# One streaming encoder step on one core: later streams in the stick-breaking attention, zero rows by VectorE, own buffers for the merge's first loads, and a re-cut final norm

## The chip, the cores and the metric

One core of a Trainium2 chip runs the whole program. Times are device microseconds (us) of that core. TensorE (PE) does the matmuls and the transposes, VectorE (DVE), ScalarE (ACT) and GpSimd (POOL) do the element work, SyncE (SP) and also ACT and POOL issue DMAs. "Fill" below is matmul work that is ready at any time and is dealt out between dependent steps so that TensorE has something to do.

## What is computed

The reference is one layer of an encoder on 1024 prompt frames and on 8 running streams of 16 new frames each (1152 rows of width 1024 in all):

```python
h = rmsnorm(x); u, va, q, k, vb = split(h @ w_in)      # 512 columns each
a = gelu(u) * (tril(w_s) @ rmsnorm(gelu(va)) + b_s)    # spatial gating, chunks of 128
z = q @ k.T / 8                                        # 8 heads of 64; streams also see 256 cached frames
log_keep = where(mask, log_sigmoid(-z), 0)             # strictly causal
between = reverse_cumsum(log_keep) - log_keep
o = where(mask, exp(log_sigmoid(z) + between), 0) @ v  # stick-breaking, no softmax
x += concat(rmsnorm(a), rmsnorm(o)) @ w_out            # the merge
x += mem_attention(rmsnorm(x))                         # 4 heads of 256, 256 memory rows
x += (silu(h2 @ w_gate) * (h2 @ w_up)) @ w_down        # hidden 2816
y = rmsnorm(x)
```

The projected k and v, the memory keys and values and the streams' normed va rows are outputs too.

## The kernel before

Every float32 matrix is split into a high and a low part (`split`, L121: an ACT cast and a DVE subtraction), and each product is three matmuls (`mm3`, L129). The rows stand in nine tiles of 128 (`NT`); tile 8 holds the streams' 128 rows. The program is written in stages, and the framework orders each engine's instructions by its own plan, near to the order in which they are written; each engine then runs its own list strictly in that order.

**Start and projections** (L208 to L380). Weights and x are loaded, x is normed and turned, and k, v, q and the two gating parts are projected. `head_in(h)` (L190) loads the operands of one attention head from scratch DRAM; for the first two heads it also writes zeros into the half of `qz` that the head does not use (L194).

**Attention** (L385 to L736). Three sources of work are interleaved:

- *Prompt chunks* (`pair`, `chunk`, `sticks`): 8 heads of 12 chunks, 96 in all. A chunk is a chain: two matmuls into `z` on PE, two sigmoids on ACT, a scan on DVE (L417), a product on POOL (L419), transposes on PE (L403), a split on ACT and DVE, and for each pair of chunks the matmuls into `av` (L472). The sum of `av`'s two halves goes to DRAM from the single-buffered tile `oe` (L476 to L479) through SP.
- *Streams* (`stream`, L509): one for each of the 8 running streams, with the same chain in plain float32, and then `stream_tails` (L554), which adds the part of the new frames: four DVE products (L560), eight float32 matmuls, eight DVE sums (L571), and a store (L573). While a stream is in its last matmuls it stands in the list `held`.
- *Fill*: `memory()` (L598), which projects the memory rows, and then `merge_a()` (L634), which computes the first half of the merge, rows of `a_d` times `w_out`. `merge_a` loads a tile's rows of `a_d` into `ar` (L640), transposes them (`prep`), and runs 24 matmuls for each row tile (accumulators `acc`, whose sums are L684). It may not start a `prep` while `held` is not empty, and then hands the turn back (`yield 1`).

`tasks()` (L700) brings the chunks and the streams in order: stream b enters when `S0 + 10 b` chunks have entered, the tails at `S0 + 80`, and the loads of stream b at `S0 + 10 (b - 1) + 8`. The loop that deals the turns counts PE cost by its own rule (`mm`: columns, at least 256, for float32r, and twice the doubled columns for float32; 261 for a transpose) and adds fill until a pass has cost `SLOT` = 4700 counts:

```python
for task in tasks():
    spent[0] = 0
    active.insert(0, task)
    active = [g for g in active if next(g, g) is not g]
    while spent[0] < SLOT:
        if next(fill, 1):
            break
```

A second loop of the same form (L729) drains what is left after the last task. Each pass lets every active chunk and stream take one step.

The outputs of `memory()` go through the tile `mo` (tag "mo", two buffers, L629), which `ar` shares in this kernel.

**Merge, memory attention, feed-forward** (L740 to L1295). The second merge half (`merge_in`, `merge`) starts with loads of `gmem` (L136) and `xt` (L753).

**End** (L1297 to L1351). The down projection runs in six rounds over the nine row tiles, two column halves of 512 each (accumulator `pd`, tag "tr", all eight PSUM banks), summed into `xr` (L1335). In the last round each half is also squared and summed by ACT into `ss` (L1340, its elementwise output is thrown away), POOL turns the two sums into the factor r (L1347, L1348), DVE multiplies the second half by the gain `gfin` (L1349), and `final` (L1312) scales and stores the tile: the first half by DVE (L1316), the second by ACT (L1319).

Of the kernel before, what the change touches and what calls it, by code (L numbers as in the profile page):

```python
# [9 lines left out]
F32 = mybir.dt.float32  # L10
F32R = mybir.dt.float32r
AF = mybir.ActivationFunctionType
ALU = mybir.AluOpType
# [3 lines left out]
P = 128  # L17
# [20 lines left out]
def stream_step(ctx: ExitStack, tc: tile.TileContext, I, O, cst):  # L38
# [14 lines left out]
    def nm(s):  # L53
        uid[0] += 1
        return f"{s}_{uid[0]}"
# [134 lines left out]
    def head_in(h):  # L190
        e, c2 = h % 2, h // 2
        es = slice(e * 64, e * 64 + 64)
        if h < 2:
            nc.gpsimd.memset(qzs[e][64 - e * 64:128 - e * 64].bitcast(F32), 0.0)  # L194
        nc.sync.dma_start(qzs[e][es].bitcast(F32), q_d[c2, 1, es, 0:NP])
        qhh = bhp.tile([P, NP], F32R, tag="qhh", name=nm("qhh"))
        khl = bhp.tile([P, NP], F32R, tag="khl", name=nm("khl"))
        for n in range(2):
            half = slice(n * 64, n * 64 + 64)
            nc.sync.dma_start(khl[half].bitcast(F32), k_d[c2, n ^ e, es, 0:NP])  # L200
            nc.sync.dma_start(qhh[half].bitcast(F32), q_d[c2, 0, es, 0:NP])
        if e == 0:
            vhl = bhp.tile([P, 8, 2, P], F32R, tag="vhl", name=nm("vhl"))
            nc.sync.dma_start(vhl.bitcast(F32), v_d[:, h:h + 2, :].rearrange("(n p) e d -> p n e d", p=P))
            vhls.append(vhl)
        got[h] = qhh, qzs[e], khl, vhls[-1]
# [178 lines left out]
    with ExitStack() as st:  # L385
# [248 lines left out]
        def merge_a():  # L634

            xs = tmp_.tile([P, 2, D], F32, tag="mt", name="xs2")
            aT = tmp_.tile([P, 2, 2, 4, P], F32R, tag="mt", name="aT2")

            def load(i):
                ar = mp.tile([P, 512], F32, tag="mo", name=nm("ar"))  # L640
                nc.sync.dma_start(ar, a_d[i * P:(i + 1) * P, :])
                xt = xs[:, i % 2]
                nc.sync.dma_start(xt, rows(x_p, x_s, i))
                return i, ar, xt

            def prep(i, ar, xt):
                tr = ps("tr", [P, 4, P])
                for c in range(4):
                    tp_(tr[:, c, :], ar[:, c * P:(c + 1) * P], ident)
                ah, al = aT[:, i % 2, 0], aT[:, i % 2, 1]  # L650
                split(ah, al, tr)
                return xt, ah, al

            ins = [load(0), load(1)]
            ws[19] = mem_split(19, raws.pop(19), pend)
            yield 1
            split(*pend.pop())
            yield 1
            while held:
                yield 1  # L660
            cur = prep(*ins.pop(0))
            yield 1
            for i in range(NT):
                xt, ah, al = cur
                if i in (1, 3, 5, 7):
                    raws[20 + i // 2] = mem_load(20 + i // 2)
                elif i in (2, 4, 6, 8):
                    ws[19 + i // 2] = mem_split(19 + i // 2, raws.pop(19 + i // 2), pend)
                for half in range(2):
                    pa = ps("acc", [P, 512])  # L670
                    cnt = 0
                    for c in range(4):
                        wh, wl = ws[16 + c]
                        for lh, rh in ((ah, wh), (ah, wl), (al, wh)):
                            mm(pa, lhsT=lh[:, c, :], rhs=rh[:, half, :], start=cnt == 0, stop=cnt == 11)
                            cnt += 1
                            if cnt % 2 == 0:
                                yield
                            if cnt >= 6 and cnt % 2 == 0 and half == 1 and ins and ins[0][0] == i + 1 and not held:
                                cur = prep(*ins.pop(0))  # L680
                            if cnt == 6 and half == 0 and pend:
                                split(*pend.pop())
                    hs = slice(half * 512, (half + 1) * 512)
                    nc.vector.tensor_tensor(out=xt[:, hs], in0=pa, in1=xt[:, hs], op=ALU.add)  # L684
                yield
                if ins and ins[0][0] == i + 1:
                    while held:
                        yield 1
                    cur = prep(*ins.pop(0))
                nc.scalar.dma_start(xa_d[i * P:(i + 1) * P, :], xt)  # L690
                if i + 2 < NT:
                    ins.append(load(i + 2))

        S0 = 4
        SLOT = 4700
        ZC = 1
        LAG = 2
# [303 lines left out]
    with ExitStack() as stE:  # L1001
# [310 lines left out]
        def final(i, r, xg):  # L1312
            for half in range(2):
                hs = slice(half * 512, (half + 1) * 512)
                if half == 0:
                    nc.vector.scalar_tensor_tensor(out=xr[i][:, hs], in0=xr[i][:, hs], scalar=r, in1=gfin[:, hs], op0=ALU.mult, op1=ALU.mult)  # L1316
                    nc.sync.dma_start(rows(y_p, y_s, i)[:, hs], xr[i][:, hs])
                else:
                    nc.scalar.activation(xr[i][:, hs], xg[:, hs], AF.Copy, scale=r)  # L1319
                    nc.scalar.dma_start(rows(y_p, y_s, i)[:, hs], xr[i][:, hs])  # L1320

        for c, fs in enumerate(chunks):
# [3 lines left out]
            for i in range(NT):  # L1326
# [3 lines left out]
                for half in range(2):  # L1330
                    hs = slice(half * 512, (half + 1) * 512)
                    pd = ps("tr", [P, 512])
                    for n, (hid, wd) in enumerate(now):
                        mm3(pd, hid[:, 0, tsl], hid[:, 1, tsl], wd[:, 0, hs], wd[:, 1, hs], n == 0, n == len(now) - 1)
                    nc.vector.tensor_tensor(out=xr[i][:, hs], in0=pd, in1=xr[i][:, hs], op=ALU.add)  # L1335
                    if last:
                        if half == 0:
                            junk = jp.tile([P, D], F32, tag="w", name=nm("junk"))
                            ss = sm(2)
                        nc.scalar.activation(junk[:, hs], xr[i][:, hs], AF.Square, scale=1.0 / 32, accum_out=ss[:, half:half + 1])  # L1340
                if loads and i % 2 == 1:
                    have.append(prep(*loads.pop(0)))
                if last:
                    if sums:
                        final(i - 1, *sums.pop())
                    tot, r = sm(), sm()
                    nc.gpsimd.tensor_scalar(out=tot, in0=ss[:, 0:1], scalar1=ss[:, 1:2], scalar2=EPS, op0=ALU.add, op1=ALU.add)  # L1347
                    nc.gpsimd.tensor_tensor(out=r, in0=tot, in1=mhalf[:, 0:1], op=ALU.pow)  # L1348
                    nc.vector.tensor_tensor(out=junk[:, hs], in0=xr[i][:, hs], in1=gfin[:, hs], op=ALU.mult)  # L1349
                    sums.append((r, junk))  # L1350
        final(NT - 1, *sums.pop())  # L1351

# [41 lines left out]
```

## Time and profile before

| | us |
| --- | --- |
| runs of the kernel before | 1740.65, 1745.07, 1749.17 (median 1745.07) |
| the profiled execution, its own time | 1748.1 |
| the profiled execution, its span | 1746.2 |

The span runs from the first to the last instruction in the trace; what lies around it in that execution is 1.9 us. Mean granted TensorE clock over the span: 0.989 of 2.4 GHz. By the windows of the trace the projections end near 288 us, the attention near 570, the second merge half near 635, the feed-forward's first products near 1463, and the rest is the down projection and the final norm. The runs shown differ by up to 0.5% of the time.

### The profile page before, as it was taken

The numbers are of one execution on the slowest core, as the hardware profiler recorded it, in microseconds if no ns is written. First come the engines' busy times: TensorE is split into PE (matmuls) and PEld (weight loads), VectorE is DVE, ScalarE is ACT, GpSimd is POOL, SyncE is SP. The second block draws the span as 40 slices with busy tenths as digits, with TensorE's granted clock in tenths as the row PEclk, the third lists the DMA queues.
The fourth block names the chain that finished last, engine by engine and source line by source line (L and its number), as shares of the span: only waits on it lengthen the run. The fifth ranks groups of instructions, "written<-read, shape, count | busy, mean of one in ns | idle before, by whom it ended". The sixth has DMA issues, their size and how long they took to land. (4 is left out here: it accounts for less than half of the span.)

```text
span 1746.2 us, 26290 instructions
## 1 busy us (share of the span) xinstructions
PE 1689.4 (97%) x10039; PEld 1499.7 (86%) x10039; DVE 982.0 (56%) x1479; ACT 676.7 (39%) x1328; POOL 431.8 (25%) x574
## 2 busy tenths in 40 slices
PE   8999999998999999999899899999999999999997
PEld 5889887777777799998788899999999999788886
DVE  5312354888778746545635865555554556444444
ACT  5322234776556436545522523323322233011123
POOL 2101223544333220000001254444444432000002
PEclk9999999999998999999899999999999999999999
DMA  8548145567744534443833232222222237222202
GB/s 272 160 163 278 61 157 170 178 201 210 210 133 159 158 110 125 126 126 113 283 109 108 68 100 70 75 70 72 76 76 77 76 102 264 103 103 103 102 13 97
DMA packets 178253, 229.51 MB, mean 131 GB/s; under 512 B 12176, under 2 KB 125456, under 8 KB 178128
## 3 DMA queue, kind: packets, MB, share of 16 engines
q1 hardware_dynamic: 146432, 163.46, 31.0%
q10 hardware_dynamic: 23504, 35.79, 5.6%
q0 software_dynamic: 8192, 28.58, 4.3%
q8 instruction: 80, 1.31, 0.3%
q14 instruction: 45, 0.37, 0.1%
HBM read 163.43 MB, written 64.36 MB: 130 GB/s over the span
## 5 line engine op out<-in xcount | busy, mean ns | idle before, releaser
L1199 PE MATMUL pp<-b,wg 128*128 128x288 f32 x1584 | 221.4, 296 | 3.4 <-ACT wg L126 2.3
L1199 PEld LDWEIGHTS pp<-b,wg 128*128 128x128 f32 x1584 | 213.5, 188 | 4.3 <-ACT wg L126 2.5
L131 PE MATMUL tr<-wd,hid 128*128 128x512 f32 x396 | 154.7, 391 | 1.2 <-DVE wd L127 1.2
L132 PE MATMUL tr<-wd,hid 128*128 128x512 f32 x396 | 154.1, 389 | 0.0
L130 PE MATMUL tr<-wd,hid 128*128 128x512 f32 x396 | 151.4, 389 | 0.0
L127 DVE TENSOR_TENSOR wg<-s,wg 128x512 fp32r<-128x512 f32 x88 | 87.8, 1000 | 99.5 <-ACT wg L126 86.4
L1335 DVE TENSOR_TENSOR xr<-tr,xr 128x512 f32<-128x512 f32 x108 | 73.2, 689 | 122.2 <-PE tr L132 116.5
L419 POOL TENSOR_TENSOR beta<-beta,pr 128x512 f32<-128x512 f32 (+4 forms) x104 | 96.7, 931 | 141.9 <-DVE pr L417 128.0
L130 PE MATMUL acc<-wh,hah 128*128 128x512 f32 x288 | 114.3, 397 | 0.0
L132 PE MATMUL acc<-wh,hal 128*128 128x512 f32 x288 | 113.3, 393 | 0.0
L131 PE MATMUL acc<-wl,hah 128*128 128x512 f32 x288 | 112.8, 392 | 0.0
L126 ACT CAST hid<-hr 128x576 fp32r<-128x576 f32 x44 | 27.5, 669 | 192.9 <-PE tr L132 178.7
L131 PEld LDWEIGHTS tr<-wd,hid 128*128 128x128 f32 x396 | 74.3, 188 | 18.1 <-DVE wd L127 2.9
L126 ACT CAST wg<-s 128x512 fp32r<-128x512 f32 x88 | 54.2, 619 | 87.4 <-DVE g L1183 43.9
L130 PEld LDWEIGHTS tr<-wd,hid 128*128 128x128 f32 x396 | 74.3, 188 | 15.9
L132 PEld LDWEIGHTS tr<-wd,hid 128*128 128x128 f32 x396 | 74.3, 188 | 15.2
L126 ACT CAST wg<-raw 128x512 fp32r<-128x512 f32 x66 | 40.5, 622 | 118.2 <-PE pp L1199 46.7
L1045 POOL DMA_DIRECT2D x_d<-xt x9 | 5.6, 624 | 309.2 <-DVE xt L1044 309.2
L127 DVE TENSOR_TENSOR wl<-raw,wh 128x1024 fp32r<-128x1024 f32 x36 | 43.7, 1222 | 47.5 <-ACT wh L126 46.5
L1347 POOL TENSOR_SCALAR sm<-sm 128x1 f32<-128x1 f32 x9 | 7.1, 794 | 251.0 <-ACT junk L1340 251.0
L399 PE MATMUL acc<-mw,aT 128*128 128x512 f32 x216 | 67.7, 426 | 1.3 <-ACT aT L126 1.3
L1111 POOL TENSOR_TENSOR s<-raw 128x512 f32<-128x512 f32 x22 | 29.1, 1322 | 156.1 <-DMA raw<-in_w_ffn_up_dram 75.9
(292 smaller groups left out, 4532.9 us busy)
## 6 DMA issues: line engine op xcount, KB each, us to landing
hr<-hid_d SPq DMA_DIRECT2D x44, 288.0 KB, 4.9
raw<-in_w_ffn_up_dram SPq DMA_DIRECT2D x24, 512.0 KB, 4.0
hid_d<-g ACTq DMA_DIRECT2D x42, 288.0 KB, 2.1
raw<-in_w_ffn_gate_dram SPq DMA_DIRECT2D x23, 512.0 KB, 3.8
raw<-in_w_ffn_down_dram SPq DMA_DIRECT2D x22, 512.0 KB, 4.3
raw<-in_w_in_dram SPq DMA_DIRECT2D x20, 512.0 KB, 5.0
x_d<-xt POOLq DMA_DIRECT2D x18, 512.0 KB, 3.4
raw<-in_cache_mem_k_dram SPq DMA_DIRECT2D x16, 512.0 KB, 4.5
```

The source lines that it names most:

```text
L126: nc.scalar.copy(hi, src)
L127: nc.vector.tensor_tensor(out=lo, in0=src, in1=hi.bitcast(F32), op=ALU.subtract)
L130: nc.tensor.matmul(out, lhsT=lh, rhs=rh, start=first, stop=False)
L131: nc.tensor.matmul(out, lhsT=lh, rhs=rl, start=False, stop=False)
L132: nc.tensor.matmul(out, lhsT=ll, rhs=rh, start=False, stop=last)
L399: nc.tensor.matmul(out, lhsT=lhsT, rhs=rhs, start=start, stop=stop)
L419: nc.gpsimd.tensor_tensor(out=beta[:, :w], in0=beta[:, :w], in1=pr[:, 1:w + 1], op=ALU.mult)
L1045: nc.gpsimd.dma_start(x2_d[i * P:(i + 1) * P, :], xt)
L1111: nc.gpsimd.tensor_tensor(out=s[n], in0=x, in1=y, op=op)
L1199: nc.tensor.matmul(acc[:, h], lhsT=hl[:, a, c], rhs=b[:, c, h * TN:(h + 1) * TN], start=c == 0 and k == 0, stop=c == 3 and k == 2)
L1335: nc.vector.tensor_tensor(out=xr[i][:, hs], in0=pd, in1=xr[i][:, hs], op=ALU.add)
L1347: nc.gpsimd.tensor_scalar(out=tot, in0=ss[:, 0:1], scalar1=ss[:, 1:2], scalar2=EPS, op0=ALU.add, op1=ALU.add)
```

## The change

Four things are edited. `S0` goes from 4 to 9, so that every stream, its loads and the tails enter five chunks later. The zero rows of `qz` are written by VectorE where GpSimd wrote them. `ar` gets its own tag and so two buffers of its own, 4 KB a partition more in that pool. In the last round of the down projection the squares are written into the accumulator `pd`, the product with `gfin` no longer shares a tile with them and is written ahead of `final` of the tile before, and its tile has 512 columns where it had 1024.

```diff
         if h < 2:
-            nc.gpsimd.memset(qzs[e][64 - e * 64:128 - e * 64].bitcast(F32), 0.0)
+            nc.vector.memset(qzs[e][64 - e * 64:128 - e * 64].bitcast(F32), 0.0)
...
             def load(i):
-                ar = mp.tile([P, 512], F32, tag="mo", name=nm("ar"))
+                ar = mp.tile([P, 512], F32, tag="ar", name=nm("ar"))
...
-        S0 = 4
+        S0 = 9
...
                 else:
-                    nc.scalar.activation(xr[i][:, hs], xg[:, hs], AF.Copy, scale=r)
+                    nc.scalar.activation(xr[i][:, hs], xg, AF.Copy, scale=r)
...
                     if last:
                         if half == 0:
-                            junk = jp.tile([P, D], F32, tag="w", name=nm("junk"))
+                            junk = jp.tile([P, 512], F32, tag="w", name=nm("junk"))
                             ss = sm(2)
-                        nc.scalar.activation(junk[:, hs], xr[i][:, hs], AF.Square, scale=1.0 / 32, accum_out=ss[:, half:half + 1])
+                        nc.scalar.activation(pd, xr[i][:, hs], AF.Square, scale=1.0 / 32, accum_out=ss[:, half:half + 1])
+                        if half == 1:
+                            nc.vector.tensor_tensor(out=junk, in0=xr[i][:, hs], in1=gfin[:, hs], op=ALU.mult)
...
                     nc.gpsimd.tensor_tensor(out=r, in0=tot, in1=mhalf[:, 0:1], op=ALU.pow)
-                    nc.vector.tensor_tensor(out=junk[:, hs], in0=xr[i][:, hs], in1=gfin[:, hs], op=ALU.mult)
                     sums.append((r, junk))
```

## Rows read from the trace of the kernel before

**Rows 1.** The page's busy times: engine, us, share of the span, instructions.
```profile
PE 1689.4 (97%) x10039; PEld 1499.7 (86%) x10039; DVE 982.0 (56%) x1479; ACT 676.7 (39%) x1328; POOL 431.8 (25%) x574
```

**Rows 2.** Windows: stretch, its length, busy by engine (instructions), granted clock, DMA share, GB/s.
```profile
400.00:405.00 5.00, 3.00 (x19) 2.06 (x17) 4.78 (x11) 3.96 (x12) 1.67 (x5) 0.98 0.88 289
405.00:410.00 5.00, 5.00 (x25) 4.42 (x25) 4.11 (x8) 2.66 (x6) 2.69 (x6) 0.68 0.38 106
440.00:445.00 5.00, 4.12 (x29) 3.12 (x26) 3.10 (x6) 2.23 (x7) 0.77 (x2) 1.00 1.04 376
445.00:450.00 5.00, 4.26 (x14) 3.46 (x15) 3.69 (x5) 2.74 (x7) 1.72 (x4) 0.66 0.97 293
540.00:545.00 5.00, 4.99 (x29) 4.15 (x28) 4.03 (x11) 2.23 (x8) 1.63 (x3) 1.00 0.44 159
550.00:555.00 5.00, 4.53 (x24) 2.81 (x22) 5.00 (x10) 4.28 (x9) 3.09 (x5) 1.00 0.83 231
555.00:560.00 5.00, 2.85 (x16) 2.22 (x15) 5.00 (x7) 3.20 (x8) 3.40 (x5) 0.84 0.95 375
560.00:565.00 5.00, 3.84 (x16) 3.43 (x17) 4.26 (x7) 2.64 (x5) 1.22 (x2) 0.50 0.86 275
565.00:570.00 5.00, 5.00 (x23) 4.37 (x22) 1.96 (x5) 2.11 (x4) 0.80 (x3) 0.63 0.32 94
```

**Rows 3.** Windows of PE's instructions on `acc` alone (the fill's matmuls).
```profile
400.00:405.00 5.00, 0.00 (x0) 0.98 0.88 289
440.00:445.00 5.00, 0.00 (x0) 1.00 1.04 376
555.00:560.00 5.00, 0.00 (x0) 0.84 0.95 375
```

**Rows 4.** The tails' DVE instructions: count, ns min/median/max, first and last start.
```profile
L560 DVE TENSOR_TENSOR wt<-tr,csb x4: 398/414/414, 528.1 to 529.1; 128x256 f32<-128x256 f32 x4
L571 DVE TENSOR_TENSOR oTs<-tr,oTs x8: 256/288/296, 535.1 to 542.7; 64x128 f32<-64x128 f32 x8
```

**Rows 5.** Waits of SP's queue in the attention: total us, times, longest.
```profile
SPq L641 <- DMA out_dram<-mo: 7.4, 2, 6.8
```

**Rows 6.** Timeline around that wait: start, us, engine, line [idle before <- releaser].
```profile
405.03 0.40 DVE L478 TENSOR_TENSOR oe<-av,oe 64x256 f32<-64x256 f32 x1
...
406.52 0.33 SPq L641 DMA_DIRECT2D ar<-a_d  x1
406.95 0.47 SPq L479 DMA_DIRECT2D oT_d<-oe  x1
...
410.12 0.37 ACT L477 COPY oe<-av 64x256 f32<-64x256 f32 x1 [0.57 <-DMA oT_d<-oe]
```

**Rows 7.** Timeline of the start: both zero fills' engines.
```profile
0.90 0.48 DVE L245 MEMSET cold<- 128x512 f32 x1 [0.90 <-PEq L1380]
...
0.92 1.94 POOL L194 MEMSET qz<- 64x1024 f32 x2
...
9.61 1.23 DVE L127 TENSOR_TENSOR wl<-raw,wh 128x1024 fp32r<-128x1024 f32 x1 [8.22 <-ACT wh L126]
```

**Rows 8.** Timeline of the last tile's final norm.
```profile
1736.91 0.63 ACT L1340 ACTIVATE junk<-xr 128x512 f32<-128x512 f32 x1 [1.03 <-DVE xr L1335]
...
1737.66 0.69 DVE L1349 TENSOR_TENSOR junk<-xr,gfin 128x512 f32<-128x512 f32 x1 [0.79 <-ACT junk L1340]
1737.73 0.79 POOL L1347 TENSOR_SCALAR sm<-sm 128x1 f32<-128x1 f32 x1 [4.00 <-ACT junk L1340]
```

**Rows 9.** POOL's one-column sums by line: ns min/median/max.
```profile
L141 POOL TENSOR_SCALAR sm<-sm x54: 220/222/1026, 5.8 to 972.0; 128x1 f32<-128x1 f32 x45, 128x4 f32<-128x4 f32 x9
L1347 POOL TENSOR_SCALAR sm<-sm x9: 786/795/797, 1696.9 to 1737.7; 128x1 f32<-128x1 f32 x9
```

**Rows 10.** Timeline at the start of the second merge half.
```profile
550.02 0.45 SPq L136 DMA_DIRECT2D gmem<-in_ln_mem_dram  x1
...
571.14 0.73 DVE L779 SCALAR_TENSOR_TENSOR xt<-acc,sm,xt 128x512 f32<-128x512 f32 x1
```

## Prediction

> **What bounds the kernel now.** I read the page's busy times first: TensorE is busy 97% of the span, VectorE 56% [rows 1]. So the time is TensorE's work plus its gaps, and an edit that removes no matmul can only win gaps back. Of the four edits one re-times the attention (300 to 570 us), one acts where the attention's fill changes from the memory projection to the merge, one at the very start, one in the last microseconds.
>
> Next I read windows of 5 us through the attention, looking for stretches in which PE idles or its granted clock is under 1.00. Three stand out: 400 to 410, 440 to 450 and 550 to 570 us [rows 2]. In each the clock falls from 2.4 toward 1.2 GHz behind a stretch in which PE idled. The windows of the fill's matmuls say why: in 400 to 405, 440 to 445 and 555 to 560 not one ran [rows 3]. Where the fill runs, the gaps are small; where it pauses, PE waits for the chain of sigmoid, scan, product and split.
>
> The price of each gap is idle time plus (1 - clock) times the length [rows 2]:
> - 400 to 410: idle 2.00, clock (0.02 + 0.32) x 5 = 1.70, together 3.7 us.
> - 440 to 450: idle 0.88 + 0.74, clock 0.34 x 5 = 1.70, together 3.3 us.
> - 550 to 570: idle 0.47 + 2.15 + 1.16 = 3.78, clock (0.16 + 0.50 + 0.37) x 5 = 5.15, together 8.9 us.
>
> Sum 15.9 us, 0.9% of the time. This is what `S0` can move.
>
> **The change part by part: S0.** The dealing loop counts its costs in the source, so its passes can be written out by hand for both values: which pass stops short of 4700 because the fill broke off. Both need 110 passes and 546,025 counts. These counts are an order of work and no time. With `S0` = 4 the short passes are 43 to 45 (memory projection done, first `prep` waits; 4307 counts short in sum), 58 to 60 (`prep` of a tile waits because a stream is held; 3539) and 102 to 110 (the fill is used up; 24,767). The three gaps of the trace lie just there: pass 43 at about 400 us and pass 102 at about 550 us make 2.5 us a pass, and pass 59 then falls on 441. So the loop's order explains the trace, and I use it for the order after.
>
> With `S0` = 9 the short passes are 42 to 44 (3253 short), 63 and 64 (2192), a new group at 85 to 87 (stream 6 is held where `prep` of tile 6 is due; 2264) and 106 to 110 (15,248). The fill lasts four passes longer into the drain, because it was held back more on the way. In sum 22,957 counts are short, where 32,613 were.
>
> Each gap of after is priced by the us per 1000 short counts of its like: 3.7 / 4.307 = 0.86, 3.3 / 3.539 = 0.94, 8.9 / 24.767 = 0.36. That gives 2.8 + 2.1 + 2.0 (the new group, taken at 0.90, between its two neighbours) + 5.5 = 12.4 us. Gain 3.5 us. Bounds: none of it (the drain takes as long as VectorE needs), or all the clock loss too (below).
>
> Against it: the tails move five chunks, about 13 us, later. Their twelve DVE instructions cost 4 x 0.41 + 8 x 0.29 = 4.0 us [rows 4]. Now most run before 543 us, where DVE is busy 4.03 of 5; after, the last eight fall in passes 101 to 104, on the stretch where DVE is busy 5.00 of 5 [rows 2]. Half of those eight's 2.3 us as delay: +1.2 us; bounds 0 and 4.0. The streams' loads move by the same five chunks on SP's queue, past loads of the heads and stores of `oe`. The order of those collisions changes and their number does not: nothing, and I leave it to the range.
>
> **Own buffers for `ar`.** Two loads of `ar` wait for the stores of `mo` today, 7.4 us in all [rows 5]. Behind the long wait on SP stands a store of `oe`, ready at 405.43 and issued at 406.95; the next ACT copy into `oe` waits 0.57 us for such a store [rows 6]. The first `ar` is not what the first `prep` waits for (its wait is the short one, 0.6 us). I take the 0.57 us: -0.5 us. Bounds 0 and -1.5 (the store's whole lateness). The pool's extra 4 KB shifts the tiles behind it; what they replace is over before, at nothing.
>
> **Zeros by VectorE.** POOL does both in 1.94 us from 0.92 on [rows 7]. On DVE, 512 columns cost 0.48 us in the same rows, so two times 1024 are 1.9 us. DVE then idles 8.22 us before its first split at 9.61 [rows 7]; that idle time hides them. POOL is not waited for there either. Zero; with the cover gone at most 1.9 us.
>
> **The end.** On the last tile the product with `gfin` must wait for the square, since both write one tile: it starts at 1737.66, when the square's sum is done, and POOL's sum starts 0.07 us later and takes 0.79 [rows 8]. POOL's other one-column sums have a median of 0.22 us [rows 9]. After, the product follows the addition directly and runs beside the square, so it is over when POOL starts. What is that worth? Either the 0.57 us between the two medians (0.795 - 0.222), if the product holds POOL up, or nothing, if two operands from memory make this form longer. All nine take 786 to 797 ns with the product beside them, so the rows can't part the two; but POOL's sum ends 0.17 us after the product does (1738.52 against 1738.35), which fits being held. I take -0.6 us; bounds 0 and -0.7.
>
> The Trainium skill, SBUF — State Buffer, section Who interferes with whom, says that a VectorE instruction with two SBUF inputs and a GpSimd instruction that reads SBUF exclude each other, the second waiting for all of the first. By that rule the sum here is -0.57 us, by the other reading of the row 0; no run so far shows which. It also speaks against the edit: for tiles 0 to 7 `final`'s scaling of the tile before now comes second and can hold POOL in its turn, which costs nothing while PE has the next tile's matmuls.
>
> **Sum.** -3.5 + 1.2 - 0.5 + 0 - 0.6 = -3.4 us. The profiled execution took 1748.1 us around a span of 1746.2, so it would take 1744.7 and its span 1742.8. That execution lies 3.0 us above the median of the runs shown, so for the median: 1745.07 - 3.4 = 1741.7, -0.2%.
>
> **The rivals.**
> - *The clock stays up* (much faster). With shorter gaps PE's clock may not fall at all, and only idle time is left: 2.00 x 3253 / 4307 = 1.5, then 1.62 x 2192 / 3539 = 1.0, 1.0 for the new group, 3.78 x 15,248 / 24,767 = 2.3, together 5.8 in place of 15.9. With the other terms: -10.1 + 1.2 - 0.5 - 0.6 = -10.0, 1735.1 us. For it: 550 to 555 us has 0.47 us of idle time at full clock. Against it: the fall at 445 follows a window with no more than 0.88 us of idle time [rows 2].
> - *The drain is VectorE's* (no change). DVE is full from 550 to 560 [rows 2]; if it sets the drain's length, fill there brings its own splits and sums to DVE and wins nothing: 2.8 + 2.1 + 2.0 + 8.9 = 15.8, and +1.2 - 1.1 leave 1745.1 us. For it: the two 5.00s. Against it: at 560 to 570 DVE is free and PE still loses 5.5 us, 4.35 of it to the clock.
> - *The second merge half starts late* (slower). `gmem` and `xt` take the place of the weights that the last `acc` matmul reads, so they can't load before the fill ends: 550.02 us now, and the first use is 571.14 [rows 10]. Four passes later is 560; the first use would be 567.7. Their 2 MB then compete with the other loads of that time (DMA share 0.95 and 0.86 [rows 2]); if they need more than 7.7 us from issue to use, PE waits. From about 11 us on the gain of 3.4 is gone; at 20 us the wait is 12.3 us, and 1741.7 + 12.3 = 1754 us.
> - *The change does not do what it says*: the plan that orders the engines may put other work into the short passes. Then the gaps are elsewhere and the outcome lies between the first two.
>
> **How the numbers follow.** The forecast and its near neighbours get 0.48, the clock that stays up 0.20, no change 0.22, the late merge 0.10. A difference of 0.5%, 8.7 us, is about what a measurement of this kernel can tell from none (the runs spread over 0.5%). Faster than that, under 1736.3: the first rival and a little of the forecast's lower side, 0.22. Slower, over 1753.8: most of the late merge, 0.08. The rest 0.70. The forecast's own range is 1737 to 1746 (the bounds of its terms half used). To hold 8 of 10 the range takes in the first rival at 1735 and the late merge's cheap half: 1733 to 1750.
>
> **What would show it.** In the profile after: no `acc` matmul for some us at about 397 to 404, 451 to 456, 507 to 515 and from about 560 on, and PE's lower clock there and nowhere else in the attention; the last L684 about 8 us later relative to the end of the attention; the tails' L571 ending near 553; no wait of L641 for `mo`; L194 on DVE before 5 us; POOL's L1347 at about 0.22 us on the last tile. The prediction is wrong if the attention's end does not move, if low clock turns up in other stretches, or if the time between 560 and 640 grows.

## The result, and the profile after

| | before | after |
| --- | --- | --- |
| median of five runs, us | 1743.26 (1740.65 to 1749.17) | 1733.99 (1731.84 to 1735.52) |
| ratio | 1 | 0.9936, 95% interval 0.9923 to 0.9949 |
| profiled execution, its span, us | 1748.1, 1746.2 | 1733.99, 1732.2 |
| mean granted TensorE clock | 0.989 | 0.995 |

The change wins 9.3 us on the medians (0.53%); the ratio on record, which is not the quotient of the two medians, says 0.64%. The two spans differ by 14.0 us, because the profiled execution of before lay 4.8 us above its median. Forecast were 3.4. Landmarks of the two traces say where the 14.0 lie. The memset behind the projections (L493), which stands for their end here, starts at 288.3 us before and at 285.6 after: 2.7 us won at the start. From there to the first query product's copy (L823), which is attention and merge, it takes 347.3 and 337.4: 9.9 us. From there to the last sum of the down projection (L1335) it is 1100.6 and 1099.6, and behind that sum's start 10.1 and 9.6.

Busy times of after, beside [rows 1]: TensorE has the same 10039 instructions and 4.2 us less busy time.
```profile
PE 1685.2 (97%) x10039; PEld 1495.1 (86%) x10039; DVE 977.5 (56%) x1481; ACT 675.0 (39%) x1328; POOL 426.6 (25%) x572
```
Windows of after in the order of [rows 2] (stretch, length, busy of PE, PEld, DVE, ACT, POOL, granted clock, DMA share, GB/s):
```profile
395.00:400.00 5.00, 4.37 (x27) 3.02 (x26) 5.00 (x10) 3.14 (x9) 1.95 (x2) 1.00 1.00 332
400.00:405.00 5.00, 5.00 (x26) 3.26 (x25) 2.55 (x6) 1.70 (x5) 1.56 (x5) 1.00 0.94 322
450.00:455.00 5.00, 3.62 (x26) 2.97 (x27) 5.00 (x9) 3.13 (x9) 2.44 (x5) 1.00 1.00 315
550.00:555.00 5.00, 4.44 (x26) 3.17 (x27) 5.00 (x10) 3.98 (x7) 1.09 (x1) 1.00 1.00 329
555.00:560.00 5.00, 5.00 (x28) 4.33 (x27) 3.87 (x6) 0.38 (x2) 2.49 (x4) 1.00 0.95 367
560.00:565.00 5.00, 4.82 (x23) 3.72 (x22) 4.21 (x6) 2.82 (x5) 1.49 (x4) 1.00 0.86 265
565.00:570.00 5.00, 4.97 (x26) 3.76 (x24) 3.87 (x5) 3.06 (x6) 1.36 (x3) 1.00 0.56 157
```
Windows of the fill's `acc` matmuls alone in after, beside [rows 3]:
```profile
395.00:400.00 5.00, 0.77 (x2) 1.00 1.00 332
450.00:455.00 5.00, 0.00 (x0) 1.00 1.00 315
555.00:560.00 5.00, 4.19 (x18) 1.00 0.95 367
560.00:565.00 5.00, 4.61 (x21) 1.00 0.86 265
```
The pauses of `acc` came where the loop's counts had put them (about 397 and 451 us), and from 555 on `acc` matmuls run where before had none. These are no longer the fill's: its last sum (L684) starts at 550.8 us, and from 550.38 on the second merge half's matmuls (operand `oh`, the high part of the attention's output) run between the chain's last steps. In before they came 10 us behind the fill's last sum. Here are that sum in before, then the first `oh` matmul in before and in after:
```profile
L684 DVE TENSOR_TENSOR xs<-acc,xs x18: 653/681/692, 416.5 to 552.1; 128x512 f32<-128x512 f32 x18
562.49 0.80 PE L130 MATMUL acc<-mw,oh 128*128 128x512 f32 x1 [0.98 <-ACT oh L126]
550.38 0.47 PE L130 MATMUL acc<-mw,oh 128*128 128x512 f32 x1
```
The granted clock stayed at 1.00, which is 2.4 GHz, in every window of 5 us from 310 to 575 us.

The start of after, beside [rows 7]:
```profile
1.66 0.91 DVE L194 MEMSET qz<- 64x1024 f32 x1 [0.27 <-issue]
2.83 0.91 DVE L194 MEMSET qz<- 64x1024 f32 x1 [0.25 <-issue]
6.89 1.28 DVE L150 SCALAR_TENSOR_TENSOR xs<-xt,sm,gmix 128x1024 f32<-128x1024 f32 x1 [3.15 <-DMA gmix<-in_ln_mix_dram]
8.23 1.10 PE L159 MATMUL tr<-csb,xs 128*128 128x128 f32 x8 [0.33 <-DVE xs L150]
9.85 2.59 DVE L127 TENSOR_TENSOR wl<-raw,wh 128x1024 fp32r<-128x1024 f32 x2 [1.68 <-ACT wh L126]
```
VectorE now norms the first x tile (L150) ahead of the weight's low part (L127); before, its list had them the other way round, as the next group, of the kernel before, shows:
```profile
10.75 1.28 DVE L150 SCALAR_TENSOR_TENSOR xs<-xt,sm,gmix 128x1024 f32<-128x1024 f32 x1
...
12.08 1.80 PE L159 MATMUL tr<-csb,xs 128*128 128x128 f32 x8 [4.95 <-DVE xs L150]
```
The last tile's norm in after, beside [rows 8]: the product (now L1342) starts with the square, and POOL's sum (now L1349) takes 0.30 us where it took 0.79 [rows 9].
```profile
1723.36 0.60 ACT L1340 ACTIVATE tr<-xr 128x512 f32<-128x512 f32 x1 [1.53 <-DVE xr L1335]
1723.36 0.69 DVE L1342 TENSOR_TENSOR junk<-xr,gfin 128x512 f32<-128x512 f32 x1
...
1724.17 0.30 POOL L1349 TENSOR_SCALAR sm<-sm 128x1 f32<-128x1 f32 x1 [4.50 <-ACT tr L1340]
```
The tails, the fill's sums and the second merge half of after, grouped by line, beside [rows 4, 10]:
```profile
L684 DVE TENSOR_TENSOR xs<-acc,xs x18: 665/680/692, 406.5 to 550.8; 128x512 f32<-128x512 f32 x18
L571 DVE TENSOR_TENSOR oTs<-tr,oTs x8: 270/284/297, 535.8 to 544.4; 64x128 f32<-64x128 f32 x8
L779 DVE SCALAR_TENSOR_TENSOR xt<-acc,sm,xt x18: 731/749/764, 557.6 to 616.0; 128x512 f32<-128x512 f32 x18
```
No wait of L641 for `mo` is left [rows 5]; the first load of `ar` now starts at 301.6 us.

### The profile page after: what moved, and what is told of

Read it like the earlier page. It is cut to its first block, busy times and chain, and to the rows that moved or that the text cites. A ratio compares the mean times of both kernels' runs of the same rounds, so it can differ in the third digit from the quotient of the medians.

```text
span 1732.2 us, 26333 instructions
## 1 busy us (share of the span) xinstructions
PE 1685.2 (97%) x10039; PEld 1495.1 (86%) x10039; DVE 977.5 (56%) x1481; ACT 675.0 (39%) x1328; POOL 426.6 (25%) x572
## 4 chain that ended last, share of the span: by engine, by line
PE 78%; DVE 6%; issue 5%; DMA 5%; ACT 3%; POOL 1%; SPq 0%; POOLq 0%; DVEq 0%; ACTq 0%
PE pp L1199 27%; PE tr L131 5%; PE acc L130 5%; PE tr L132 5%; PE tr L130 5%; PE acc L132 5%; PE acc L131 5%; PE acc L399 4%; PE tr L403 2%; PE z L399 2%; PE pp L130 2%; PE av L399 2%; PE pp L131 2%; PE pp L132 2%; DMA or<-oT_d 1%
## 5 line engine op out<-in xcount | busy, mean ns | idle before, releaser
L1335 DVE TENSOR_TENSOR xr<-tr,xr 128x512 f32<-128x512 f32 x108 | 73.2, 690 | 124.7 <-PE tr L132 120.3
L127 DVE TENSOR_TENSOR wg<-s,wg 128x512 fp32r<-128x512 f32 x88 | 79.6, 906 | 97.1 <-ACT wg L126 84.2
L127 DVE TENSOR_TENSOR wg<-raw,wg 128x512 fp32r<-128x512 f32 x66 | 60.5, 918 | 12.3 <-ACT wg L126 12.3
L127 DVE TENSOR_TENSOR wl<-raw,wh 128x1024 fp32r<-128x1024 f32 x36 | 43.9, 1223 | 40.7 <-ACT wh L126 39.5
```

Of the source, the lines that this page charges most:

```text
L127: nc.vector.tensor_tensor(out=lo, in0=src, in1=hi.bitcast(F32), op=ALU.subtract)
```

## The experiments

All were timed in five rounds against the kernel before. The groups e1 to e4, e5 to e8, e9 to e12, e13 to e15, e16 to e17 and e18 each had their own runs of before, with medians from 1742.5 to 1746.3 us; rows of different groups are therefore compared by their ratios. The last column is read from one trace of each kernel: "to the fill's end" is the time from the projections' end to the start of the last sum of the fill (L684), "gap" from there to the start of the first sum of the second merge half (L779), "att + merge" from the projections' end to L823. The expectations below give some gaps up to 2.3 us too short, since they count from the wait ahead of that sum. The pass in which the fill ends follows from the loop's counts.

| kernel | S0, fill ends in pass | median us, ratio [95%] | to the fill's end, gap, att + merge |
| --- | --- | --- | --- |
| before (profiled) | 4, 102 | | 263.9, 19.0, 347.3 |
| after | 9, 106 | 1733.99, 0.9936 [0.9923, 0.9949] | 265.3, 6.8, 337.4 |
| e1 zeros only | 4, 102 | 1742.72, 0.9981 [0.9970, 0.9992] | 263.9, 17.8, 346.5 |
| e2 S0 only | 9, 106 | 1738.64, 0.9961 [0.9947, 0.9974] | 266.2, 6.6, 339.3 |
| e3 `ar` only | 4, 102 | 1744.66, 0.9998 [0.9989, 1.0007] | 263.3, 16.8, 343.9 |
| e4 end only | 4, 102 | 1743.33, 0.9989 [0.9976, 1.0002] | 262.5, 17.0, 343.4 |
| e5 before, SLOT 4600 | 4, 110 | 1742.75, 0.9994 [0.9985, 1.0003] | 271.7, 5.9, 342.4 |
| e6 after, SLOT 4600 | 9, 109 | 1735.51, 0.9952 [0.9939, 0.9965] | 269.0, 6.9, 340.3 |
| e7 after, S0 = 11 | 11, 106 | 1743.31, 0.9995 [0.9987, 1.0004] | 272.1, 8.3, 348.2 |
| e8 after, S0 = 8 | 8, 101 | 1739.37, 0.9969 [0.9957, 0.9981] | 256.6, 19.1, 340.7 |
| e9 zeros on both | 4, 102 | 1747.33, 1.0014 [1.0003, 1.0025] | 261.9, 19.0, 345.6 |
| e10 after, late 4900 | 9, 100 | 1740.62, 0.9971 [0.9959, 0.9984] | 257.1, 20.7, 342.9 |
| e11 before, late 4400 | 4, 106 | 1740.75, 0.9978 [0.9969, 0.9988] | 271.7, 4.2, 342.1 |
| e12 S0 = 8, late 4500 | 8, 105 | 1736.93, 0.9960 [0.9945, 0.9975] | 266.5, 8.5, 339.5 |
| e13 after, long pause | 9, 106 | 1732.69, 0.9935 [0.9919, 0.9952] | 264.2, 6.8, 336.2 |
| e14 after, short pause | 9, 106 | 1737.65, 0.9966 [0.9952, 0.9979] | 268.8, 6.8, 341.8 |
| e15 after, S0 = 4, short pause | 4, 106 | 1736.84, 0.9959 [0.9945, 0.9973] | 277.3, 4.2, 346.7 |
| e16 before, late 4400, short pause | 4, 104 | 1740.08, 0.9967 [0.9956, 0.9979] | 265.5, 12.2, 341.6 |
| e17 before, late 4500, long pause | 4, 106 | 1736.08, 0.9949 [0.9932, 0.9966] | 266.5, 6.0, 337.3 |
| e18 e17 with the other three edits | 4, 106 | 1732.87, 0.9932 [0.9916, 0.9949] | 268.4, 6.0, 339.5 |

**The four edits one by one** (e1 to e4, each one of the four edits on the kernel before).

> The kernel before with the two zero fills on VectorE and nothing else changed. Theory A (with the fills off GpSimd the plan places the first norm's scaling ahead of the first weight split on VectorE, and the first projections start earlier): 2 to 3 us faster, ratio about 0.9985, the first transposes of x near 8.2 us where they stood at 12.1, and no lower clock removed from the attention. Rival B (the start moved because of another edit): ratio 1.000, first transposes at 12.1 us.

> The kernel before with S0 = 9 and nothing else changed. Theory A (the order of streams and fill sets the gaps): 5 to 8 us faster, ratio 0.9955 to 0.997; no clock under 0.9 in 550 to 575 us, and the windows without fill near 400, 452 and 505 us. Rival B (the gaps went because ar's loads no longer queue behind mo's stores): under 2 us, the gap near 400 us as wide as before and its clock low.

> The kernel before with ar's own buffers and nothing else changed. Theory A: 0 to 2 us faster (ratio 0.999 to 1.000); the wait of ar's load for mo's store gone, the gaps near 400, 440 and 550 to 570 us still there with low clock. Rival B: 4 us or more, with the gap near 400 us closed.

> The kernel before with the four edits of the final norm and nothing else changed. Theory A: 0.5 to 1.6 us faster (0.4 us behind the last addition, up to 1.2 us at the start of the down projection where tiles move in memory), ratio 0.999 to 0.9997. Rival B: the start of the down projection is unchanged and only 0.4 us is won, ratio 0.9998.

The deficits of the four ratios add up to 0.71%, the whole change has 0.64%. `S0` alone is the largest part; the zeros, which I had priced at nothing, are the second. The drain in e4, which has the attention of before, and in e2, which has `S0` = 9 (windows as above, e4 first):
```profile
550.00:555.00 5.00, 3.33 (x17) 1.96 (x16) 5.00 (x9) 4.11 (x9) 2.79 (x3) 1.00 0.91 279
555.00:560.00 5.00, 3.79 (x16) 3.10 (x16) 4.61 (x7) 2.81 (x7) 3.40 (x4) 0.66 1.04 379
```
```profile
555.00:560.00 5.00, 4.88 (x29) 3.91 (x28) 5.00 (x8) 2.53 (x4) 0.80 (x2) 1.00 0.87 298
560.00:565.00 5.00, 3.81 (x17) 2.82 (x15) 2.04 (x5) 0.91 (x2) 1.44 (x3) 1.00 1.09 348
```
Near 400 and 440 us, e4's clock stays at 1.00 where before fell to 0.68 and 0.66 [rows 2], with the same order of instructions on every engine (the second stretch in e4):
```profile
440.00:445.00 5.00, 2.73 (x19) 1.87 (x17) 2.13 (x5) 1.92 (x5) 0.77 (x2) 1.00 1.06 397
445.00:450.00 5.00, 4.53 (x23) 3.35 (x23) 4.72 (x7) 3.54 (x9) 2.35 (x5) 1.00 0.77 218
```
So part of my 15.9 us was that one execution.

**Fill that reaches into the drain, by another knob and by other positions** (e5 to e8).
```diff
-        SLOT = 4700
+        SLOT = 4600
...
-        S0 = 9
+        S0 = 11
```
The first hunk alone is e5 on the kernel before and e6 on the kernel after; the second alone, on the kernel after, is e7, and with 8 in place of 11 it is e8.

> The kernel before with SLOT 4600 in place of 4700; the streams stay where they are (S0 = 4). By the loop's own rule a pass then takes less fill, the fill lasts to pass 110 where it ended in pass 102, and 10,539 counts are short where 32,613 were. Theory A (fill that reaches into the drain keeps the clock up; where the streams stand matters only through that): no window under 0.95 granted clock between 550 and 575 us, acc matmuls in 560 to 570, and 4 to 7 us faster than before, ratio 0.996 to 0.9975. Rival B (it is the streams' and tails' own later place that won, by moving their chains into the drain): the drain's low clock stays and the time is that of before within 2 us, ratio 0.999 to 1.001.

> The kernel after with SLOT 4600. By the loop's rule the fill lasts to pass 109 with 11,853 counts short, where after has 106 and 22,957. Theory A, with the clock already up everywhere in after: only idle time is left to win, 1 to 3 us below after, 1731 to 1733 us, ratio 0.9925 to 0.993 to before. Rival B: no difference from after within 1 us. If the streams still held at pass 98 push the last fill out, the two groups of short passes at 75 and 98 to 99 show acc-free windows near 480 and 535 us.

> The kernel after with S0 = 11 in place of 9. By the loop's rule 106 passes of fill and 23,561 short counts, as after (106; 22,957). Theory A: the time of after within 2 us, about 1734, ratio 0.993 to 0.995, no low clock between 550 and 575 us. Rival B (the later, the better): 1 to 3 us below after.

> The kernel after with S0 = 8 in place of 9: the streams stand one chunk earlier. By the loop's rule the fill then ends in pass 101, even a pass before that of the kernel before (102), and 29,976 counts are short. Theory A: low clock is back in the drain (0.5 to 0.7 in at least one window between 545 and 570 us) and it takes 4 to 7 us more than after, 1738 to 1741 us, ratio 0.9965 to 0.9985 (what the zero rows and the end give is left). Rival B (the streams' place itself): one chunk of ninety-six changes little, within 1.5 us of after, ratio 0.993 to 0.995.

Only e8 came out as theory A had it. e6 lies 2.8 us above after by the ratios, outside of both its expectations. In e5 the gap closed (5.9 us) and the drain's low clock went, but the fill's end came 8 us later, and the clock fell at 575 to 580 us, where TensorE waited in the second merge half (a window of e5):
```profile
575.00:580.00 5.00, 3.24 (x10) 2.62 (x11) 3.10 (x7) 1.49 (x3) 2.20 (x5) 0.73 0.62 198
```
e7 has about as many counts short as after (23,561 beside 22,957) and yet takes about 10 us more by the ratios (its profiled execution lies 3.5 us above its median): 272.1 us to the fill's end and 67.8 us from L779 to L823, where before takes 64.4 and after 65.4. The sum of short counts is not the price. (A smaller `SLOT` also thins the passes ahead of 400 us, so e5 and e6 don't move the drain alone.)

**The drain alone** (e10 to e12): the fill's share is changed only behind a late pass.
```diff
-        for task in tasks():
+        for npass, task in enumerate(tasks(), 1):
+            SLOT = 4900 if npass >= 66 else 4700
```
So it stands in e10, on the kernel after. e11 has 4400 from pass 66 on the kernel before, e12 has 4500 from pass 50 on the kernel after with `S0` = 8.

> The kernel after (S0 = 9), but from pass 66 on a pass is filled up to 4900 counts where it was 4700. The streams, the tails and the fill's change-over at pass 42 stay as they are; the fill is used up in pass 100 in place of 106 (27,914 counts short behind it, where 15,248 were; the groups at 63 to 64 and 42 to 44 stay, that at 85 to 87 goes). Theory A (fill in the drain is what counts): a pause of acc matmuls of 10 us or more and low clock in the drain, 10 us or more from the last fill sum to the first sum of the second merge half (after: 6.7), 4 to 7 us slower than after, 1738 to 1741 us. Rival B (what counts is where the streams stand, S0 = 9 being good): within 2 us of after, 1733 to 1736.

> The kernel before (S0 = 4), but from pass 66 on a pass is filled up to 4400 counts where it was 4700. Nothing changes up to there (the pauses near 400 and 440 us stay, 4307 and 3539 counts short), and the fill lasts to pass 106 as in after (12,724 short, where 24,767 were). Theory A: no low clock between 550 and 570 us, 6 to 8 us from the last fill sum to the first sum of the second merge half (16 to 18 in all kernels with S0 = 4 and 4700), 3 to 5 us faster than before, ratio 0.997 to 0.9985. Rival B: as before, ratio 0.999 to 1.001.

> The kernel after with S0 = 8 and, from pass 50 on, 4500 counts a pass. With S0 = 8 and 4700 throughout it took 1739.4 us: its change-over was short (1732 counts) but its fill ended in pass 101. Now the change-over stays at 1732, the fill lasts to pass 105 (15,917 counts short behind it, after: 15,248). Theory A (change-over plus drain make the difference between these kernels): the 5 us come back, 1733 to 1735 us, ratio 0.993 to 0.9945, drain without low clock. Rival B (S0 = 9 itself): it stays at 1738 to 1740.

In e10 everything up to pass 65 is as in after; behind it a pass takes up to 200 counts more of fill, the short group at 85 to 87 goes, and the fill ends six passes sooner. The gap of before came back: 20.7 us, `acc` without work from 545 to 555, the clock at 0.66. Windows of e10, then of its `acc` matmuls:
```profile
545.00:550.00 5.00, 2.38 (x9) 1.43 (x10) 4.90 (x10) 1.52 (x4) 1.98 (x4) 1.00 0.99 312
550.00:555.00 5.00, 4.43 (x19) 3.27 (x17) 4.90 (x8) 4.06 (x9) 2.51 (x6) 0.66 0.99 337
```
```profile
545.00:550.00 5.00, 0.00 (x0) 1.00 0.99 312
550.00:555.00 5.00, 0.00 (x0) 0.66 0.99 337
```
Its fill's last sum, the second merge half's first `oh` matmul and its sums (L779 is L780 here):
```profile
L684 DVE TENSOR_TENSOR xs<-acc,xs x18: 655/677/693, 406.3 to 543.2; 128x512 f32<-128x512 f32 x18
557.19 0.48 PE L130 MATMUL acc<-mw,oh 128*128 128x512 f32 x1
L780 DVE SCALAR_TENSOR_TENSOR xt<-acc,sm,xt x18: 729/751/752, 563.9 to 622.0; 128x512 f32<-128x512 f32 x18
```
It costs 5.5 us of attention and merge against after, and 0.35% of the whole. The other way round, e11 takes the drain's gap from the kernel before and wins 0.22%. Its windows, then the same three lines:
```profile
555.00:560.00 5.00, 4.18 (x25) 3.11 (x24) 5.00 (x7) 3.53 (x6) 2.17 (x2) 1.00 0.78 237
560.00:565.00 5.00, 5.00 (x33) 4.41 (x32) 4.89 (x9) 1.35 (x3) 2.49 (x4) 1.00 0.83 256
```
```profile
L684 DVE TENSOR_TENSOR xs<-acc,xs x18: 658/674/692, 414.9 to 559.6; 128x512 f32<-128x512 f32 x18
557.71 0.48 PE L130 MATMUL acc<-mw,oh 128*128 128x512 f32 x1
L780 DVE SCALAR_TENSOR_TENSOR xt<-acc,sm,xt x18: 736/751/754, 563.9 to 623.1; 128x512 f32<-128x512 f32 x18
```
e12 closes e8's gap as well (19.1 to 8.5 us), but its fill ends 9.9 us later, and of the 0.33% that e8 lacked to after it wins back 0.09%, within the intervals. Over all runs: of the eight traces whose fill ends in pass 104 or earlier, seven have a granted clock under 0.75 between 545 and 570 us (all but e16, with pass 104); of the twelve with pass 105 or later, none. From the fill's last sum to the first `oh` matmul 10.2 to 14.0 us pass in those seven, 2.6 in e16, 3.7 in e7 and at most 0.5 in the other eleven. Idle time plus lost clock from 545 to 575 us are 5.0 to 8.9 us in the seven and 1.6 to 3.6 in all others. So the drain's loss shrinks in every kernel whose fill lasts until the second merge half can take over; whether the whole kernel gains by it depends on the rest of the attention, as e5 and e12 show.

**The pause at the change-over, and whether `S0` itself matters** (e13 to e18). "Long pause" hands back three more turns between the memory projection and the merge's first transposes; "short" one fewer (two in e14). e14 and e15 stand on the kernel after (e15 with `S0` = 4) and have 4600 counts up to pass 54.
```diff
             split(*pend.pop())
-            yield 1
+            for _ in range(4):
+                yield 1
```
This is e13 on the kernel after, and e17 on the kernel before with `SLOT` 4500 from pass 66; e18 is e17 with the other three edits of the change. e16 lacks the line taken out here, on the kernel before with 4400 from pass 66.

> The kernel after with three more turns handed back between the end of the memory projection and the merge's first transposes. By the loop's rule the change-over is then 8,690 counts short in passes 42 to 46 (after: 3,253 in 42 to 44), the groups at 63 to 64 and 85 to 87 all but go, and the end stays exactly as in after (fill to pass 106, 15,248 short). Theory A (one long run of passes without fill costs idle time and clock): 5 to 7 us lost between 400 and 450 us where after lost 2.2, 2.5 to 5 us slower than after, 1736.5 to 1739. Rival (the change-over does not matter, the drain alone made the difference): within 1.5 us of after.

> The kernel after without the two turns handed back ahead of the merge's first transposes, and with 4600 counts a pass up to pass 54: the change-over is 868 short in pass 46, 323 in pass 87, and the end stays exactly as in after (pass 106, 15,248). Theory A: 1 to 2 us lost between 400 and 450 us, up to 1.5 us faster than after, 1732.5 to 1734. Rival (the transposes, dealt without a turn between, make PE wait for the split in place of the pause): equal to after or 1 to 2 us slower.

> The kernel after with S0 = 4 again, but with the fill arranged otherwise to the same effect: one turn fewer handed back at the change-over and 4600 counts a pass up to pass 54. By the loop's rule its short groups are 2,010 in pass 49, 2,110 in pass 71 and the end exactly as in after (pass 106, 15,248). Theory A (S0 = 9 won by where the fill breaks off and nothing else): 1733 to 1736 us, no low clock between 400 and 575 us. Rival B (the streams and tails five chunks later win in themselves): 1738 to 1741, which is what the other three edits leave with S0 = 4.

> The kernel before (S0 = 4, none of the other edits) with 4400 counts a pass from pass 66 on, and one turn fewer handed back ahead of the merge's first transposes. By the loop's rule its two pauses near 400 and 440 us (4,307 and 3,539 short) shrink to one of 1,163 in passes 43 to 44, and 2,071 fall short in pass 93; the fill lasts to pass 104 (17,649 short), where the same kernel with both pauses had 106 (12,724) and took 1740.75 us. Theory P (with S0 = 4 these pauses are what the 400 to 450 us stretch loses, 5 to 8 us): 2 to 3 us lost there, 2 to 4 us faster than that kernel, 1736.5 to 1738.5. Rival Q (the streams' place sets that loss whatever the fill does, as the longer pause with S0 = 9 cost nothing): 5 us or more lost there, 1740 to 1743.

> The kernel before (S0 = 4, none of the other edits) with 4500 counts a pass from pass 66 on, and three more turns handed back ahead of the merge's first transposes. By the loop's rule it has one long pause of 10,769 in passes 43 to 49 in place of the two of 4,307 and 3,539, and the fill lasts to pass 106 (13,224 short; with both pauses: 106, 12,724, 1740.75 us). Theory P: 7 to 10 us lost between 400 and 450 us, 1 to 3 us slower than that kernel, 1742 to 1744. Rival Q: 5 to 6 us lost there, as with the two pauses, 1739.5 to 1741.5.

> The fill of the run with S0 = 4 and one long pause (10,769 counts short in passes 43 to 49, fill to pass 106; it took 1736.1 us with none of the other edits), together with the other three edits of after. Theory T (the drain's fill is what the streams' later place brought; the rest adds up): 2.7 us less for the start and about 1 us for the end, 1731.5 to 1734 us, ratio 0.991 to 0.9935, as fast as after or faster with the streams where they were. Rival B (the streams' place five chunks later is needed): 1737 us or more.

Theory A fell on the pause. e13 has more than twice after's missing counts at the change-over and is as fast. e17, with three windows in a row without one `acc` matmul, is faster than e16, where the pauses are all but gone (by the medians of one group 4.0 us; e16's fill also ends two passes sooner, so this pair doesn't show the pause alone). Two runs fit neither of their theories: e14, with hardly a pause left, is 0.30% slower than after, and e15 lies between A and B. Idle time and lost clock from 400 to 450 us are 2.2 in after, 2.0 in e13, 7.0 in e11, 4.5 in e16 and 5.5 in e17: rival Q had this stretch nearly right (5 or more in e16, 5 to 6 in e17), though e17 came out faster than either theory. But the streams' place is not what sets the whole, as e17 and e18 show. The `acc` matmuls of e17, then its drain:
```profile
400.00:405.00 5.00, 0.00 (x0) 1.00 0.72 249
405.00:410.00 5.00, 0.00 (x0) 1.00 0.43 115
410.00:415.00 5.00, 0.00 (x0) 1.00 1.01 390
```
```profile
555.00:560.00 5.00, 5.00 (x30) 4.12 (x28) 5.00 (x8) 2.17 (x3) 1.80 (x3) 1.00 0.92 309
560.00:565.00 5.00, 5.00 (x27) 4.24 (x27) 3.60 (x8) 2.15 (x4) 1.94 (x6) 1.00 1.05 345
```
And `S0` = 9 is not needed: e17, the kernel before with its streams where they were, has the attention time of after (337.3 us), and e18, which adds the other three edits, has its time (0.9932 beside 0.9936). It is no better version than after: the intervals overlap.

**The start** (e9): on the kernel before, VectorE's memset is written ahead of GpSimd's, which stays.

```diff
+            nc.vector.memset(qzs[e][64 - e * 64:128 - e * 64].bitcast(F32), 0.0)
             nc.gpsimd.memset(qzs[e][64 - e * 64:128 - e * 64].bitcast(F32), 0.0)
```


> The kernel before with the zero rows written twice, first by VectorE, then by GpSimd as before (one more pair of memsets, the same zeros). In the two runs with the zeros on VectorE alone the start came forward: xs ahead of wl on VectorE, first transposes of x near 8 us, projections over 2.7 us earlier. Theory G (GpSimd's memsets, being in the engines' plan, pushed the first x tile back): they are still there, so the start stays as before, first transposes of x at 11.5 to 12.5 us, projections over at 287.5 to 288.5, ratio 0.999 to 1.001. Theory V (VectorE's two memsets fill its queue, so the plan puts xs ahead of wl): first transposes at 8 to 9 us, projections over near 285.7, 2 to 3 us faster, ratio 0.998 to 0.9988.

The start of e9:
```profile
2.70 0.95 POOL L195 MEMSET qz<- 64x1024 f32 x1 [1.83 <-DVE qz L194]
2.84 0.91 DVE L194 MEMSET qz<- 64x1024 f32 x1 [0.27 <-issue]
...
9.70 2.60 DVE L127 TENSOR_TENSOR wl<-raw,wh 128x1024 fp32r<-128x1024 f32 x2 [5.95 <-ACT wh L126]
12.22 1.28 DVE L150 SCALAR_TENSOR_TENSOR xs<-xt,sm,gmix 128x1024 f32<-128x1024 f32 x1
```
With GpSimd's memsets back, the x tile stands behind two weight parts and waits till 12.22 us, though VectorE idles 5.95 us ahead of them. The projections end at 291.5 us. Theory V is refuted: VectorE's two memsets do not bring x forward by themselves. Theory G is right on the order, and its range is not: the start came 3.2 us later than in before, where G had no change, and the kernel is 0.14% slower. x is late in the traces with GpSimd's memsets (before, e9) and early in those without (e1, after); why it came still later in e9 is not shown.

## Why the prediction was wrong, step by step

The sign was right, and the wide range (1733 to 1750 us) held the time by 1 us, the narrower one (1737 to 1746) did not; the size was about a third of what came. Two steps of it failed.

**"Each gap of after is priced by the us per 1000 short counts of its like."** This gave 12.4 us for the gaps after, in place of 15.9. By the same rule (idle time plus lost clock) after's stretches, where the forecast put its pauses, measure 0.63 + 0.00 at 395 to 405 us, 1.38 at 450 to 455, 0.36 at 500 to 515, and 0.56 + 0.00 + 0.18 + 0.03 from 550 to 570: 3.1 us. The lost clock, 8.55 of the 15.9, was not smaller but gone. That is the rival "the clock stays up", which I gave 0.20 and priced at 5.8 us of gaps. Its total, 10.0 us, lies nearest to the 9.3 measured, in part by luck: it had the gaps too dear and nothing for the start. What I held against it, no more than 0.88 us of idle time ahead of the fall at 445, was misread: the window's border cuts a wait of 1.34 us (below). In the drain the step was mis-sized, 0.8 measured for 5.5. At the change-over it was wrong in kind: e13 lengthens the pause and loses nothing by it, and e17, with 10,769 missing counts there, loses less from 400 to 450 us than e11 with 7,846 in its two pauses. TensorE was busy 3.65 to 4.21 of 5 us in e17's three windows without `acc`, with the streams' and chunks' own work.

The price itself, idle time plus lost clock, is too high as well. Between before and after 12.8 us of it went in these stretches, and attention and merge became only 9.9 us shorter. From L493 to L823 idle time plus lost clock fell from 30.5 to 16.8 us, while the rest of that time, TensorE's busy time at full clock, rose from 316.8 to 320.7 with nearly the same matmuls (1858 TensorE instructions in that stretch of after, 1854 in before's); why it rose is not shown.

What is shown: the drain's cover is worth 3 us (e11 against the 343.4 to 347.3 us, mean 345.3, of the five traces with before's loop counts: before, e1, e3, e4, e9) to 5.5 (e10 against after). 4 to 5 us of idle time and lost clock went from 545 to 575 us in both pairs (5.7 in e10, 1.7 in after; 7.1 in the mean of the five, 2.2 in e11). `S0` = 9 was one way to get it. What stays open: among the kernels whose fill reaches pass 105 or later, attention and merge take from 336.2 to 348.2 us, a wider spread than the two pairs' differences. It comes by idle time and lost clock scattered over 285 to 500 us (12.0 to 22.5 us), by the second merge half and by TensorE's busy time. Short counts don't foretell it (e7, e15), nor does `S0` (e15, e18), nor the pauses. I have no rule for it.

**"Zeros by VectorE: zero."** Here I took the orders of the engines as fixed and asked only for cover. The end of the projections came 2.7 us earlier, in e1 2.6. The x tile can be normed from 6.9 us on (6.64 in e1, once GpSimd has its factor; 6.89 in after, once the gain `gmix` has landed); before, it stood in VectorE's list behind `wl`, which waited for ScalarE's cast until 9.61 [rows 7]. The Trainium skill, PSUM — Partial Sum Buffer, section Engine vs sequencer instructions, says that the element engines' queues are strictly first in, first out; the trace agrees, with a list's head that waited 8.22 us. That the plan reckons GpSimd's memsets longer than they are, and so takes x for late, would explain the order; that is argued from e1 and e9 and not shown.

**The other terms.** The tails (+1.2) cost nothing that shows: they ran from 535.8 to 544.7 us, ahead of the drain, and TensorE was busy 5.00 of 5 from 540 to 545. I had put them on the full stretch by passes of 2.5 us; in after the passes came sooner, and the fill, which I had ending near 560 us, had its last sum at 550.8. `ar`'s buffers (-0.5): e3 shows -0.02% with an interval of 0.09% to either side. The end (-0.6): 0.5 us in the trace, in e4 alone as well. POOL's sum lost 0.49 us in after and in e4, and what is left to the 0.22 of the other sums, 0.08, fits the two operands from memory. The Trainium skill, SBUF — State Buffer, section Who interferes with whom, has VectorE with two SBUF inputs and a GpSimd instruction that reads SBUF exclude each other; the trace agrees, with 0.79 us beside the product and 0.30 without it. The loss feared for tiles 0 to 7 isn't there: the nine sums have a median of 0.30 us and a longest of 0.48.

**The rivals.** "The drain is VectorE's" is refuted: VectorE is at 5.00 of 5 from 550 to 560 in e11 as before, and TensorE gains all the same. "The second merge half starts late" came in small part: from L779 to L823 it takes 66.2 us in e14, 66.3 in e11, 66.6 in e2 and 67.8 in e7, and 63.8 to 65.4 in the sixteen others. Before takes 64.4 and after 65.4, so after gave back 1 us there.

## What to carry to other kernels

Independent work that covers a dependent chain was worth most here at the chain's end: see to it that it lasts until the next stage's own work can start, and move it there directly (a smaller share per pass late on) before moving the chains. An instruction on an idle engine is not free when a plan orders the lists: look which list changed, not only who is busy. And test a proportional price (so much per missing count) on two sizes before using it; here the smaller gaps cost 3.1 us where the price in proportion gave 12.4.

## What was not expected of the hardware

The clock did not fall by the amount of idle time in one 5 us window. In e4, TensorE was busy 2.73 of 5 us at 440 to 445 and the next window had 1.00; in before it was busy 4.12 in that window and the next had 0.66 [rows 2]. The borders of the windows hide the waits themselves: in before a wait of 1.34 us lies across 445 us and the clock falls at its end, and in e4 a wait of 2.03 us from 443.02 on is followed by no fall. The matmul behind the wait in before:
```profile
445.74 1.63 PE L399 MATMUL acc<-mw,aT 128*128 128x512 f32 x3 [1.34 <-ACT aT L126]
```
Between executions with one order of work the clock near 400 us was 0.68 (before), 0.77 and 0.55 (e1) and 1.00 (e4). In the drain it fell in all five traces with before's loop counts.
